# The second FFN projection as one Strassen step, with its operand sums made during the first projection

## The chip, the cores and the metric

The kernel is one program on one core of a Trainium2 chip. Its time is the device time in microseconds (us) of one execution: 2015.59 us, the median of 3 runs (2013.15 to 2016.86). The engines are TensorE (PE in the rows; PEld is its weight load), VectorE (DVE), ScalarE (ACT), GpSimd (POOL) and SyncE (SP), which here only issues DMA transfers. The granted clock of TensorE has two levels, 1.2 and 2.4 GHz; in the rows 1.00 is the upper one and 0.50 the lower.

## The reference

One layer of a decoder trunk works on x with 1024 tokens and 1024 columns. Four token mixers come first; then a feed-forward network (FFN) and a gated embedding:

```
h2 = rmsnorm(x, g_pre_ffn[l])
gt, up = jnp.split(h2 @ w_ffn_in[l], 2, axis=-1)
x = x + rmsnorm((jax.nn.silu(gt) * up) @ w_ffn_out[l], g_post_ffn[l])
e = p[l] @ w_ple_in[l]
ge = jax.nn.sigmoid(rmsnorm(x, g_ple[l]) @ w_ple_gate[l])
x = x + ge * e
```

The hidden width is 2816, that is 22 tiles of 128, counted by f. Everything is float32.

## The kernel before, in words

Every matrix product is made of three matmuls in fp32r (`mm3`, L162): each operand is kept as a high part and the rest, and the kernel adds high by high, high by low and low by high. The high part is a copy on ScalarE (L74), the low part a subtraction on VectorE (L75). One matmul has a stationary tile of 128x128 and moves 512 columns.

The first projection (`ffn_in`, `ffn_in_fast`) works through f = 0 to 21 with tokens in two halves of 512. f = 0 and 1 are done plainly, 96 matmuls each: gate and up for both halves (names `fg`, `fu`), with the weights `whi`/`wlo` in two rotating buffers. Beside them `sums_of_h2` (L898) loads quarters of the normalised input (`r`, L907), forms their sums (L909 to L912) and splits them into `th`/`tl`. From f = 2 on, one Strassen step makes gate and up of a tile by 7 products of 12 matmuls (name `fw`). The sums of the weights (`sw`) and their splits (`wsh`/`wsl`) are made by `prep(f + 1)`, one step of it after each product of f. The finished hidden tile is split and stored to DRAM (`hidh`, `hidl`), 256 KB at a time.

The second projection (`ffn_out`) takes the hidden tiles in chunks of four f (the last has two). For a chunk it loads `fhh`, `fhl` and the rows of the second weight (512 KB each), and for each of 8 token tiles and 2 column halves it makes 12 matmuls into one bank (name `fo`); the sum is kept in `acc` in SBUF, copied by ScalarE for the first chunk (L1016), added by VectorE for the others (L1018). The last chunk is interleaved with the output norm and the gated embedding.

The order in each engine's queue is not that of the code: when the program is built, a planner that estimates durations and arrivals places the instructions, and each engine then works strictly in that order. Tiles of a kind share a pool of buffers (38 of 4 KB per partition for `u` tiles, 6 for `t`, 8 for `t2`, 2 each for `raw`, `whi`, `wlo`), and who takes a buffer waits for its last reader.

Of the kernel before, what the change touches and what calls it, by code (L numbers as in the profile page):

```python
# [27 lines left out]
CF_K = 31  # L28
LAG = 2
NF = HID // P  # L30
PLAIN, CHUNK = 2, 4
EPS = 1e-6
LAM_INIT = 0.8 - 0.6 * math.exp(0.0)
C_Q, C_K, C_V, C_LX, C_LG, C_SB, C_SC, C_SX, C_CA, C_CG, C_GATE = [512 * i for i in range(11)]
# [5 lines left out]
def tile_hybrid_layer(ctx: ExitStack, tc: tile.TileContext, a):  # L40
# [826 lines left out]
    acc = [None] * NT  # L867
    w1 = a["w_ffn_in"][0]
    w2 = a["w_ffn_out"][0]
    chunks = [list(range(c, min(c + CHUNK, NF))) for c in range(0, NF, CHUNK)]  # L870
    hidh, hidl = [dram.tile([NF, P, S], F32, name=n) for n in ("hidh", "hidl")]

    def keep_hidden(f, h, v):
        s = slice(h * HF, (h + 1) * HF)
        hh, hl = t2tile("fh", F32R), t2tile("fl", F32R)
        split(hh, hl, v)
        nc.sync.dma_start(hidh[f, :, s], hh.bitcast(F32))
        nc.sync.dma_start(hidl[f, :, s], hl.bitcast(F32))

    def ffn_in(f):  # L880

        gh, gl = load_w(w1[:, f * P:(f + 1) * P])
        uh, ul = load_w(w1[:, HID + f * P:HID + (f + 1) * P])
        for h in range(2):
            pg = mmtile("fg")
            mm3(pg, [(gh[:, k, :], gl[:, k, :], h2T.his(k, h * HF, HF), h2T.los(k, h * HF, HF)) for k in range(NK)])
            g = t2tile("fsilu")
            nc.scalar.activation(g, pg, AF.Silu)
            pu = mmtile("fu")
            mm3(pu, [(uh[:, k, :], ul[:, k, :], h2T.his(k, h * HF, HF), h2T.los(k, h * HF, HF)) for k in range(NK)])  # L890
            nc.vector.tensor_mul(g, pu, g)
            keep_hidden(f, h, g)

# [71 lines left out]
    def ffn_in_fast(f, ops, todo):  # L965
        x = {"B11": quarter(0, 0), "B21": quarter(1, 0), "B22": quarter(1, 1),
             "T1": tops[0], "T2": tops[1], "T3": tops[2], "T4": tops[3]}
        b0, b1, b2, b3 = banks(f, "fw")

        def product(ps, w, m, start):  # L970
            wh, wl = ops[w]
            mm3(ps, [(wh[:, k, :], wl[:, k, :], x[m][k // 2][0][:, k % 2, :], x[m][k // 2][1][:, k % 2, :])
                     for k in range(4)], start, True, not start)
            if todo:
                todo.pop(0)()

        product(b0, "A11", "B11", True)
        p1 = t2tile("p1")
        nc.scalar.activation(p1, b0, AF.Copy)
        product(b1, "S2", "T2", True)  # L980
        u2 = t2tile("u2")
        nc.vector.tensor_add(u2, b1, p1)
        product(b2, "S3", "T3", True)
        v = t2tile("v")
        nc.vector.tensor_add(v, b2, u2)
        product(b3, "S1", "T1", True)
        nc.vector.tensor_add(v, b3, v)
        product(b0, "A12", "B21", False)
        g0 = gp.tile([P, HF], F32, tag="g", name=nm("fsilu"))
        nc.scalar.activation(g0, b0, AF.Silu)  # L990
        product(b2, "A22", "T4", False)
        c21 = t2tile("c21")
        nc.vector.tensor_add(c21, b2, u2)
        nc.vector.tensor_mul(c21, c21, g0)
        keep_hidden(f, 0, c21)
        product(b3, "S4", "B22", False)
        run(todo)
        nc.vector.tensor_add(u2, b3, u2)
        g1 = gp.tile([P, HF], F32, tag="g", name=nm("fsilu"))
        nc.scalar.activation(g1, u2, AF.Silu)  # L1000
        nc.vector.tensor_mul(v, v, g1)
        keep_hidden(f, 1, v)

    def ffn_out(ci, hid, wts):
        first, last = ci == 0, ci == len(chunks) - 1
        n = len(hid)
        for t in range(NT):
            ts = slice(t * P, (t + 1) * P)
            if first:
                acc[t] = utile([P, D], F32, "acc")  # L1010
            for c in range(2):
                cs = slice(c * HF, (c + 1) * HF)
                ps = pta.tile([P, HF], F32, tag="tr" if c == 1 and not last else "ta", name=nm("fo"))
                mm3(ps, [(hid[i][0][:, ts], hid[i][1][:, ts], wts[i][0][:, cs], wts[i][1][:, cs]) for i in range(n)])
                if first:
                    nc.scalar.activation(acc[t][:, cs], ps, AF.Copy)  # L1016
                else:
                    nc.vector.tensor_add(acc[t][:, cs], acc[t][:, cs], ps)  # L1018
            if last:
                if t < 2:  # L1020
                    wpg.extend(load_row(a["w_ple_gate"][0][k * P:(k + 1) * P, :], [P, D]) for k in range(4 * t, 4 * t + 4))
                ffn_post(t)
                if t >= LAG:
                    ple(t - LAG)
        if last:
            for t in range(NT - LAG, NT):
                ple(t)
# [53 lines left out]
    for ci, fs in enumerate(chunks):  # L1081
        hid, wts = [], []
        for f in fs:
            hh, hl = utile([P, S], F32R, "fhh"), utile([P, S], F32R, "fhl")
            nc.sync.dma_start(hh.bitcast(F32), hidh[f])
            nc.sync.dma_start(hl.bitcast(F32), hidl[f])
            hid.append((hh, hl))
            wts.append(load_row(w2[f * P:(f + 1) * P, :], [P, D]))
        if ci < len(chunks) - 1:
            ffn_out(ci, hid, wts)  # L1090
# [41 lines left out]
```

## Time and profile before

| what | value |
|---|---|
| median of 3 runs | 2015.59 us |
| the profiled execution | 2013.32 us, span 2011.5 us |
| TensorE busy | 1971.7 us, 98% |
| VectorE busy | 1159.8 us, 58% |
| ScalarE busy | 755.8 us, 38% |
| mean granted clock | 0.997 |
| bytes moved by DMA | 181.10 MB, mean 90 GB/s |

The profile is of one execution. Its span is from the first to the last instruction; 1.8 us of the execution lie outside it. A matmul's row tells how long it is in the array, but matmuls overlap, so TensorE's pace is the distance between starts, and a stretch of rows without idle time gives it as its length over its count. An engine that is not the bottleneck may idle at no cost.

### The profile page before, as it was taken

The numbers are of one execution on the slowest core, as the hardware profiler recorded it, in microseconds if no ns is written. First come the engines' busy times: TensorE is split into PE (matmuls) and PEld (weight loads), VectorE is DVE, ScalarE is ACT, GpSimd is POOL, SyncE is SP. The second block draws the span as 40 slices with busy tenths as digits, with TensorE's granted clock in tenths as the row PEclk, the third lists the DMA queues.
The fourth block names the chain that finished last, engine by engine and source line by source line (L and its number), as shares of the span: only waits on it lengthen the run. The fifth ranks groups of instructions, "written<-read, shape, count | busy, mean of one in ns | idle before, by whom it ended". The sixth has DMA issues, their size and how long they took to land.

```text
span 2011.5 us, 23079 instructions
## 1 busy us (share of the span) xinstructions
PE 1971.7 (98%) x9165; PEld 1635.4 (81%) x9165; DVE 1159.8 (58%) x1663; ACT 755.8 (38%) x1251; POOL 53.7 (3%) x33
## 2 busy tenths in 40 slices
PE   6999999999999999999999999999999999999999
PEld 5878887888887888878888878888888888788887
DVE  4487679697957323464233454876666651433574
ACT  5456564511115212464122344433333332201274
POOL 1011111000000000000000000000000000000000
PEclk9999999999999999999999999999999999999999
DMA  6110111021110112112111354533333344543232
GB/s 238 61 58 22 32 32 32 22 58 48 53 53 27 58 47 63 43 32 63 48 48 47 101 183 132 176 126 109 101 126 105 105 159 165 193 180 150 85 126 94
DMA packets 185610, 181.10 MB, mean 90 GB/s; under 512 B 8112, under 2 KB 151409, under 8 KB 185502
## 3 DMA queue, kind: packets, MB, share of 16 engines
q1 hardware_dynamic: 180320, 171.47, 26.0%
q10 hardware_dynamic: 5182, 8.16, 1.2%
q8 instruction: 72, 1.18, 0.2%
q14 instruction: 36, 0.29, 0.0%
HBM read 138.96 MB, written 40.63 MB: 89 GB/s over the span
## 4 chain that ended last, share of the span: by engine, by line
PE 79%; DVE 8%; DMA 2%; ACT 2%; issue 1%; POOL 0%; SPq 0%; POOLq 0%; DVEq 0%; ACTq 0%
PE fw L171 6%; PE fw L173 6%; PE fw L174 6%; PE pg L174 5%; PE pg L173 5%; PE pg L171 5%; PE pz L171 5%; PE pz L173 5%; PE pz L174 5%; PE fo L174 4%; PE fo L173 4%; PE fo L171 4%; PE pb L174 3%; PE pb L171 3%; PE pb L173 3%; DVE cfc L473 1%
## 5 line engine op out<-in xcount | busy, mean ns | idle before, releaser
L75 DVE TENSOR_TENSOR wlo<-raw,whi 128x1024 fp32r<-128x1024 f32 x110 | 117.3, 1067 | 273.5 <-ACT whi L74 273.4
L74 ACT ACTIVATE whi<-raw 128x1024 fp32r<-128x1024 f32 (+1 forms) x128 | 121.9, 953 | 370.4 <-PE pg L173 123.4
L171 PE MATMUL pz<-hTh,whi 128*128 128x512 f32 x576 | 228.0, 396 | 2.0 <-ACT scc L609 1.7
L173 PE MATMUL pz<-hTl,whi 128*128 128x512 f32 x576 | 226.8, 394 | 0.0
L174 PE MATMUL pz<-hTh,wlo 128*128 128x512 f32 x576 | 226.5, 393 | 0.0
L174 PE MATMUL pg<-hTh,wlo 128*128 128x512 f32 x512 | 199.1, 389 | 0.5 <-DVE wlo L75 0.5
L173 PE MATMUL pg<-hTl,whi 128*128 128x512 f32 x512 | 199.3, 389 | 0.0
L171 PE MATMUL pg<-hTh,whi 128*128 128x512 f32 x512 | 199.2, 389 | 0.0
L473 DVE SCALAR_TENSOR_TENSOR cfc<-cfu,cvec,cfc 128x994 f32<-128x994 f32 (+14 forms) x120 | 161.3, 1344 | 2.6
L171 PE MATMUL fo<-rwh,fhh 128*128 128x512 f32 x352 | 136.4, 390 | 0.7 <-DMA fhh<-hidh 0.5
L173 PE MATMUL fo<-rwl,fhh 128*128 128x512 f32 x352 | 136.4, 390 | 0.2
L174 PE MATMUL fo<-rwh,fhl 128*128 128x512 f32 x352 | 135.8, 389 | 0.0
L171 PEld LDWEIGHTS pz<-hTh,whi 128*128 128x128 f32 x576 | 108.9, 189 | 25.2 <-ACT scc L609 2.2
L174 PEld LDWEIGHTS pz<-hTh,wlo 128*128 128x128 f32 x576 | 108.9, 189 | 22.8 <-issue 0.5
L173 PEld LDWEIGHTS pz<-hTl,whi 128*128 128x128 f32 x576 | 108.9, 189 | 22.3 <-issue 0.7
L1018 DVE TENSOR_TENSOR acc<-acc,fo 128x512 f32<-128x512 f32 x80 | 54.6, 687 | 104.1 <-PE fo L174 104.1
L174 PEld LDWEIGHTS pg<-hTh,wlo 128*128 128x128 f32 x512 | 96.1, 188 | 20.9 <-DVE wlo L75 0.9
L171 PEld LDWEIGHTS pg<-hTh,whi 128*128 128x128 f32 x512 | 96.1, 188 | 19.9
L173 PEld LDWEIGHTS pg<-hTl,whi 128*128 128x128 f32 x512 | 96.1, 188 | 19.8
L74 ACT ACTIVATE rwh<-raw 128x1024 fp32r<-128x1024 f32 x40 | 41.8, 1058 | 175.8 <-PE fo L173 109.7
L171 PE MATMUL fw<-th,wsh 128*128 128x512 f32 x240 | 93.4, 389 | 0.0
L173 PE MATMUL fw<-tl,wsh 128*128 128x512 f32 x240 | 93.4, 389 | 0.0
(319 smaller groups left out, 4181.0 us busy)
## 6 DMA issues: line engine op xcount, KB each, us to landing
raw<-in_w_in_dram SPq DMA_DIRECT2D x72, 512.0 KB, 3.6
raw<-in_w_ffn_in_dram SPq DMA_DIRECT2D x44, 512.0 KB, 3.7
hidh<-fh SPq DMA_DIRECT2D x44, 256.0 KB, 2.8
hidl<-fl SPq DMA_DIRECT2D x44, 256.0 KB, 2.2
raw<-in_w_ffn_out_dram SPq DMA_DIRECT2D x22, 512.0 KB, 7.8
fhh<-hidh SPq DMA_DIRECT2D x22, 512.0 KB, 3.6
fhl<-hidl SPq DMA_DIRECT2D x22, 512.0 KB, 7.9
raw<-in_w_branch_dram SPq DMA_DIRECT2D x32, 256.0 KB, 2.8
```

The lines of the kernel that those rows point to most:

```text
L74: nc.scalar.activation(dst_hi, src, AF.Copy)
L75: (eng or nc.vector).tensor_sub(dst_lo, src, dst_hi.bitcast(F32))
L171: nc.tensor.matmul(ps, lhsT=lh, rhs=rh, start=start and i == 0, stop=False, skip_group_check=onto)
L173: nc.tensor.matmul(ps, lhsT=lh, rhs=rl, start=False, stop=False, skip_group_check=onto)
L174: nc.tensor.matmul(ps, lhsT=ll, rhs=rh, start=False, stop=stop and i == n - 1, skip_group_check=onto)
L473: nc.vector.scalar_tensor_tensor(o, in0=src[:, a0 - sh:t0 + n - sh], scalar=cv(name, j, k), in1=o, op0=ALU.mult, op1=ALU.add)
L1018: nc.vector.tensor_add(acc[t][:, cs], acc[t][:, cs], ps)
```

## The change

The first ten pairs of tiles f (0 to 19) of the second projection are done by one Strassen step: tokens in two halves, output columns in two halves, and the two f of a pair as the two halves of the inner dimension. For a pair, 7 products take the place of 8; each has 4 token tiles of 3 matmuls. Pairs are taken in groups of 3, 3 and 4, whose products are summed in the same bank. The seven left operands of a pair (A11, A12, A22 and four sums HS1 to HS4 of the hidden quarters) are made and split in the first projection, in steps (`spare`) of which one is taken after each product, and stored to DRAM (`sums_d`, 36.7 MB, where `hidh` and `hidl` held 21.0 MB for these twenty tiles). The second projection (`out_fast`) loads one of them (`so`, 512 KB) for each pair and product, forms and splits the weight's sums (`to`) as it goes, and adds the products into `acc` and, for two of them, `accu`. The tiles f = 20 and 21 stay as they were (`out_last`). The hidden tile now stays in SBUF in a `t` buffer (`hid`) until its pair's sums are made.

```diff
-PLAIN, CHUNK = 2, 4
+PLAIN, NP = 2, 10
+GROUPS = (3, 3, 4)
...
+    sums_d = dram.tile([7, NP, P, 2, HF], F32, name="sums_d")
+    last_d = dram.tile([NF - 2 * NP, 2, P, S], F32, name="last_d")
+    A11, A12, A22, HS1, HS2, HS3, HS4 = range(7)
+    hidden, spare = {}, []
+    def keep(dst, v):
         hh, hl = t2tile("fh", F32R), t2tile("fl", F32R)
         split(hh, hl, v)
-        nc.sync.dma_start(hidh[f, :, s], hh.bitcast(F32))
-        nc.sync.dma_start(hidl[f, :, s], hl.bitcast(F32))
+        nc.sync.dma_start(dst[0], hh.bitcast(F32))
+        nc.sync.dma_start(dst[1], hl.bitcast(F32))
+    def keep_hidden(f, h):
+        n, second = divmod(f, 2)
...
+        if h == 0:
+            spare.append(lambda: put(A12 if second else A11, hidden[f][:, 0]))
+        elif second:
+            x, y, z = hidden[f - 1], hidden[f], []
+            def first():
+                z.append(utile([P, 2, HF], F32, "hs"))
+                nc.vector.tensor_add(z[0][:, 0], x[:, 1], y[:, 1])
+                nc.vector.tensor_sub(x[:, 1], x[:, 0], x[:, 1])
+            def then():
+                nc.vector.tensor_sub(z[0][:, 1], z[0][:, 0], x[:, 0])
+                nc.vector.tensor_sub(y[:, 0], y[:, 0], z[0][:, 1])
+            spare.extend([lambda: put(A22, y[:, 1]), first, lambda: put(HS3, x[:, 1]), then,
+                          lambda: put(HS1, z[0][:, 0]), lambda: put(HS2, z[0][:, 1]), lambda: put(HS4, y[:, 0])])
     def ffn_in(f):
...
+        hidden[f] = ttile(S, "hid").rearrange("p (u c) -> p u c", u=2)
...
-            nc.vector.tensor_mul(g, pu, g)
-            keep_hidden(f, h, g)
+            nc.vector.tensor_mul(hidden[f][:, h], pu, g)
+            keep_hidden(f, h)
...
             if todo:
                 todo.pop(0)()
+            if spare:
+                spare.pop(0)()
...
+    order = (("P1", A11), ("P6", HS2), ("P2", A12), ("P7", HS3), ("P5", HS1), ("P4", A22), ("P3", HS4))
+    onto = {"P2": "P1", "P4": "P7", "P3": "P5"}
...
+    def out_ops(g, name, i):
+        for n in members[g]:
+            so = utile([P, 2, HF], F32R, "so")
+            nc.sync.dma_start(so.bitcast(F32), sums_d[i, n])
...
+            to = utile([P, 2, HF], F32R, "to")
+            split(to[:, 0], to[:, 1], src[0][:, src[1]])
...
+    def out_fast():
+        seq = [(g, name, i) for g in range(len(GROUPS)) for name, i in order]
...
+        for m, (g, name, i) in enumerate(seq):
+            ops = nxt
+            if name == "P4" and g + 1 < len(GROUPS):
+                load_raw(g + 1)
+            if m + 1 < len(seq):
+                nxt = out_ops(*seq[m + 1])
...
+            for t in range(NH):
+                ts = slice(t * P, (t + 1) * P)
+                mm3(ps[t], [(s[:, 0, ts], s[:, 1, ts], w[:, 0], w[:, 1]) for s, w in ops], not cont, True, cont)
...
+                if g == 0 and name not in ("P6", "P5"):
+                    nc.scalar.activation(dst, ps[t], AF.Copy)
+                else:
+                    nc.vector.tensor_add(dst, dst, ps[t])
+                if g == len(GROUPS) - 1 and name in ("P4", "P5", "P3"):
+                    nc.vector.tensor_add(dst, dst, accu[t])
```

The change also moves instructions. Three places at the handover from the plain tiles (f = 0, 1) to the fast ones (f = 2) are shown, of before and of the change. On VectorE, this is the stretch ahead of the second product of f = 2, before (`r` are the input's sums of the second set, `wlo` the low part of the plain first operand's weights of f = 2, `wsl` that of the second product's, `fu` the up half of f = 1):

```order
L911 TENSOR_TENSOR r_1683_9857<-r_1683_9857,r_1681_9853 128x1024
L75 TENSOR_TENSOR tl_1686_9866<-r_1681_9853,th_1685_9865 128x1024
L912 TENSOR_TENSOR r_1684_9859<-r_1684_9859,r_1683_9857 128x1024
L891 TENSOR_TENSOR fsilu_1672_9760<-fu_1673_9762,fsilu_1672_9760 128x512
L75 TENSOR_TENSOR tl_1688_9870<-r_1683_9857,th_1687_9869 128x1024
L75 TENSOR_TENSOR tl_1690_9874<-r_1682_9855,th_1689_9873 128x1024
...
L939 TENSOR_TENSOR sw_1696_9886<-raw_1693_9881,sw_1695_9885 128x512
L75 TENSOR_TENSOR wlo_1698_9890<-raw_1693_9881,whi_1697_9889 128x1024
L75 TENSOR_TENSOR wsl_1700_9896<-sw_1695_9885,wsh_1699_9895 128x1024
```

and the same work on VectorE in the change:

```order
L942 TENSOR_TENSOR r_1675_9831<-r_1676_9833,r_1675_9831 128x1024
L76 TENSOR_TENSOR wlo_1692_9868<-raw_1687_9859,whi_1691_9867 128x1024
L943 TENSOR_TENSOR r_1676_9833<-r_1677_9835,r_1676_9833 128x1024
L76 TENSOR_TENSOR tl_1680_9844<-r_1675_9831,th_1679_9843 128x1024
L944 TENSOR_TENSOR r_1677_9835<-r_1677_9835,r_1675_9831 128x1024
L924 TENSOR_TENSOR hid_1668_9724<-fu_1674_9805,fsilu_1673_9803 128x512
L945 TENSOR_TENSOR r_1678_9837<-r_1678_9837,r_1677_9835 128x1024
L76 TENSOR_TENSOR tl_1682_9848<-r_1677_9835,th_1681_9847 128x1024
...
L971 TENSOR_TENSOR sw_1689_9863<-sw_1689_9863,raw_1687_9859 128x512
...
L76 TENSOR_TENSOR wsl_1694_9874<-sw_1689_9863,wsh_1693_9873 128x1024
```

`wlo` has moved from behind the second set of input sums to a place after the first of them; between it and `wsl` now stand 13 other instructions, where there was none. On SP, the DMA issues before:

```order
L907 DMA r_1681_9853<-h2d_8746 128x2x512
L907 DMA r_1682_9855<-h2d_8746 128x2x512
L907 DMA r_1683_9857<-h2d_8746 128x2x512
L927 DMA raw_1693_9881<-in_w_ffn_in_dram 128x8x128
L907 DMA r_1684_9859<-h2d_8746 128x2x512
```

and in the change:

```order
L960 DMA raw_1687_9859<-in_w_ffn_in_dram 128x8x128
L960 DMA raw_1688_9861<-in_w_ffn_in_dram 128x8x128
L940 DMA r_1675_9831<-h2d_8746 128x2x512
L940 DMA r_1676_9833<-h2d_8746 128x2x512
L940 DMA r_1677_9835<-h2d_8746 128x2x512
L940 DMA r_1678_9837<-h2d_8746 128x2x512
```

The second set of input quarters is now issued behind both weight tiles of f = 2 (the two `hid` tiles hold two of the six `t` buffers that it used). On TensorE, this is the end of the first product of f = 2 and the start of the second (before, `fw_1704` is the bank of the first and `fw_1705` that of the second; in the change `fw_1698` and `fw_1699`; `h2Th_1471` belongs to the fifth product, which adds onto the first one's bank). Before:

```order
L171 MATMUL fw_1704_9906<-h2Th_1470_8731,whi_1697_9889 128x512
L173 MATMUL fw_1704_9906<-h2Tl_1478_8739,whi_1697_9889 128x512
L174 MATMUL fw_1704_9906<-h2Th_1470_8731,wlo_1698_9890 128x512
L171 MATMUL fw_1705_9907<-th_1659_9711,wsh_1699_9895 128x512
L173 MATMUL fw_1705_9907<-tl_1660_9712,wsh_1699_9895 128x512
L174 MATMUL fw_1705_9907<-th_1659_9711,wsl_1700_9896 128x512
```

and in the change:

```order
L175 MATMUL fw_1698_9884<-h2Th_1470_8731,wlo_1692_9868 128x512
L172 MATMUL fw_1698_9884<-h2Th_1471_8732,whi_1691_9867 128x512
L174 MATMUL fw_1698_9884<-h2Tl_1479_8740,whi_1691_9867 128x512
L172 MATMUL fw_1699_9885<-th_1656_9700,wsh_1693_9873 128x512
L174 MATMUL fw_1699_9885<-tl_1657_9701,wsh_1693_9873 128x512
L175 MATMUL fw_1698_9884<-h2Th_1471_8732,wlo_1692_9868 128x512
L175 MATMUL fw_1699_9885<-th_1656_9700,wsl_1694_9874 128x512
```

Three matmuls of the fifth product have moved ahead of the third matmul of the second, which is the first to read `wsl`.

## Rows read from the trace of the kernel before

**Rows 1.** The page: the span, and busy time per engine.
```profile
span 2011.5 us, 23079 instructions
PE 1971.7 (98%) x9165; PEld 1635.4 (81%) x9165; DVE 1159.8 (58%) x1663; ACT 755.8 (38%) x1251; POOL 53.7 (3%) x33
```

**Rows 2.** Stretches (each engine's busy us and count, granted clock, DMA): both projections.
```profile
core 0: us, PE busy (x) PEld busy (x) DVE busy (x) ACT busy (x) POOL busy (x), PEclk, DMA share, GB/s
1400.00:1437.90 37.90, 37.90 (x169) 31.39 (x168) 25.46 (x35) 13.36 (x18) 0.00 (x0) 1.00 0.34 111
1724.00:1832.30 108.30, 108.30 (x479) 89.71 (x478) 41.54 (x54) 11.46 (x11) 0.00 (x0) 1.00 0.45 171
1669.90:1886.70 216.80, 216.11 (x951) 178.06 (x950) 69.25 (x89) 32.03 (x39) 0.00 (x0) 1.00 0.40 149
```

**Rows 3.** Groups by form in 1724.00 to 1832.30.
```profile
L174 PE MATMUL fo<-rwh,fhl 128*128 128x512 f32 x160 | 62.2, 389 | 0.0
L1018 DVE TENSOR_TENSOR acc<-acc,fo 128x512 f32<-128x512 f32 x43 | 29.4, 687 | 66.5 <-PE fo L174 66.5
```

**Rows 4.** Timeline of TensorE at the handover to f = 2.
```profile
1283.20 0.39 PE L171 MATMUL fu<-h2Th,whi 128*128 128x512 f32 x1
...
1288.64 0.39 PE L171 MATMUL fw<-h2Th,whi 128*128 128x512 f32 x1
1288.86 0.39 PE L173 MATMUL fw<-h2Tl,whi 128*128 128x512 f32 x1
...
1291.36 0.39 PE L171 MATMUL fw<-th,wsh 128*128 128x512 f32 x1
...
1291.81 0.39 PE L174 MATMUL fw<-th,wsl 128*128 128x512 f32 x1
```

**Rows 5.** Timeline of VectorE at the handover.
```profile
1277.54 1.22 DVE L911 TENSOR_TENSOR r<-r,r 128x1024 f32<-128x1024 f32 x1
1278.68 1.22 DVE L75 TENSOR_TENSOR tl<-r,th 128x1024 fp32r<-128x1024 f32 x1
...
1285.55 0.69 DVE L933 TENSOR_TENSOR sw<-raw,raw 128x512 f32<-128x512 f32 x1
1286.15 0.69 DVE L938 TENSOR_TENSOR sw<-sw,raw 128x512 f32<-128x512 f32 x1
...
1287.49 1.22 DVE L75 TENSOR_TENSOR wlo<-raw,whi 128x1024 fp32r<-128x1024 f32 x1
1288.62 2.35 DVE L75 TENSOR_TENSOR wsl<-sw,wsh 128x1024 fp32r<-128x1024 f32 x2
```

**Rows 6.** Timeline of ScalarE at the handover.
```profile
1283.22 1.06 ACT L74 ACTIVATE whi<-raw 128x1024 fp32r<-128x1024 f32 x1
```

**Rows 7.** The stretch of the handover.
```profile
1268.30:1288.60 20.30, 20.30 (x91) 16.84 (x90) 18.57 (x20) 9.63 (x12) 0.00 (x0) 1.00 0.41 130
```

**Rows 8.** Timeline of TensorE after an idle time near the kernel's start.
```profile
27.81 0.79 PE L171 MATMUL pe<-whi,pTh 128*128 128x512 f32 x1 [4.84 <-ACT e L220]
28.40 0.63 PE L173 MATMUL pe<-wlo,pTh 128*128 128x512 f32 x1
28.83 0.63 PE L174 MATMUL pe<-whi,pTl 128*128 128x512 f32 x1
...
33.45 0.40 PE L173 MATMUL pe<-wlo,pTh 128*128 128x512 f32 x1
33.69 0.40 PE L174 MATMUL pe<-whi,pTl 128*128 128x512 f32 x1
```

**Rows 9.** Stretches around that idle time.
```profile
23.00:28.00 5.00, 0.19 (x1) 0.19 (x2) 2.42 (x4) 4.33 (x8) 0.00 (x0) 0.81 0.94 318
28.00:32.00 4.00, 4.00 (x10) 3.02 (x11) 1.73 (x2) 1.47 (x3) 0.94 (x1) 0.50 1.00 364
18.00:20.00 2.00, 2.00 (x14) 1.74 (x13) 0.62 (x2) 1.22 (x3) 0.95 (x1) 1.00 1.01 396
```

**Rows 10.** DMA issues: count, KB each, median us to landing.
```profile
raw<-in_w_ffn_out_dram SPq DMA_DIRECT2D x22, 512.0 KB, 7.8
```

More of the change, by code (lines that the diff above doesn't have):

```diff
@@ L869, in tile_hybrid_layer, with put @@
     w2 = a["w_ffn_out"][0]
[L870 to L874, printed above, removed]
+    sums_d = dram.tile([7, NP, P, 2, HF], F32, name="sums_d")
[3 more added lines that the diff above has]
+    def keep(dst, v):
         hh, hl = t2tile("fh", F32R), t2tile("fl", F32R)
         split(hh, hl, v)
-        nc.sync.dma_start(hidh[f, :, s], hh.bitcast(F32))
-        nc.sync.dma_start(hidl[f, :, s], hl.bitcast(F32))
+        nc.sync.dma_start(dst[0], hh.bitcast(F32))
+        nc.sync.dma_start(dst[1], hl.bitcast(F32))
+    def keep_hidden(f, h):
+        n, second = divmod(f, 2)
+        if n >= NP:
+            s = slice(h * HF, (h + 1) * HF)
+            spare.append(lambda: keep([last_d[f - 2 * NP, u, :, s] for u in range(2)], hidden[f][:, h]))
+            return
+        def put(i, v):
+            keep([sums_d[i, n, :, u, :] for u in range(2)], v)
+        if h == 0:
[11 more added lines that the diff above has]
+                          lambda: put(HS1, z[0][:, 0]), lambda: put(HS2, z[0][:, 1]), lambda: put(HS4, y[:, 0])])
     def ffn_in(f):
@@ L975, in product @@
                 todo.pop(0)()
+            if spare:
+                spare.pop(0)()
+        hv = ttile(S, "hid").rearrange("p (u c) -> p u c", u=2)
+        hidden[f] = hv
         product(b0, "A11", "B11", True)
@@ L991, in ffn_in_fast @@
         product(b2, "A22", "T4", False)
[L992 to L995, printed above, removed]
+        nc.vector.tensor_add(hv[:, 0], b2, u2)
+        nc.vector.tensor_mul(hv[:, 0], hv[:, 0], g0)
+        keep_hidden(f, 0)
         product(b3, "S4", "B22", False)
@@ L1000, in ffn_in_fast @@
         nc.scalar.activation(g1, u2, AF.Silu)
[L1001 to L1006, printed above, removed]
+        nc.vector.tensor_mul(hv[:, 1], v, g1)
+        keep_hidden(f, 1)
+    NH = NT // 2
+    order = (("P1", A11), ("P6", HS2), ("P2", A12), ("P7", HS3), ("P5", HS1), ("P4", A22), ("P3", HS4))
+    onto = {"P2": "P1", "P4": "P7", "P3": "P5"}
+    sets = {"P1": 0, "P6": 1, "P7": 1, "P5": 0}
@@ new lines, in tile_hybrid_layer, with load_raw @@
+    raws, mids = {}, {}
+    def load_raw(g):
+        for n in members[g]:
+            raws[n] = []
+            for f in (2 * n, 2 * n + 1):
+                raws[n].append(utile([P, 2, HF], F32, "w2r"))
+                nc.sync.dma_start(raws[n][-1], w2[f * P:(f + 1) * P, :].rearrange("p (u c) -> p u c", u=2))
+    def out_ops(g, name, i):
+        ops = []
+        for n in members[g]:
+            so = utile([P, 2, HF], F32R, "so")
+            nc.sync.dma_start(so.bitcast(F32), sums_d[i, n])
+            ops.append([so])
+        for n, op in zip(members[g], ops):
+            (r0, r1) = raws[n]
+            if name == "P6":
+                m = mids[n] = ttile(D, "tt").rearrange("p (u c) -> p u c", u=2)
+                nc.vector.tensor_sub(m[:, 0], r0[:, 1], r0[:, 0])
+                nc.vector.tensor_sub(m[:, 1], r1[:, 1], m[:, 0])
+            elif name == "P7":
+                nc.vector.tensor_sub(r0[:, 1], r1[:, 1], r0[:, 1])
+            elif name == "P4":
+                nc.vector.tensor_sub(mids[n][:, 1], r1[:, 0], mids[n][:, 1])
+            src = {"P1": (r0, 0), "P2": (r1, 0), "P7": (r0, 1), "P3": (r1, 1)}.get(name)
+            if src is None:
+                src = (mids[n], 0 if name == "P5" else 1)
+            to = utile([P, 2, HF], F32R, "to")
+            split(to[:, 0], to[:, 1], src[0][:, src[1]])
+            op.append(to)
+        return ops
@@ new lines, in tile_hybrid_layer @@
+    members, n0 = [], 0
+    for n in GROUPS:
+        members.append(list(range(n0, n0 + n)))
+        n0 += n
+    accu = []
+    def out_fast():
+        seq = [(g, name, i) for g in range(len(GROUPS)) for name, i in order]
+        for t in range(NT):
+            acc[t] = utile([P, D], F32, "acc")
+        for t in range(0, NH, 2):
+            u = utile([P, 2, HF], F32, "accu")
+            accu.extend([u[:, 0], u[:, 1]])
+        lo, hi = slice(0, HF), slice(HF, D)
+        load_raw(0)
+        nxt = out_ops(*seq[0])
+        held = {}
+        for m, (g, name, i) in enumerate(seq):
[4 more added lines that the diff above has]
+                nxt = out_ops(*seq[m + 1])
+            cont = name in onto
+            if cont:
+                ps = held[onto[name]]
+            else:
+                ps = held[name] = banks(g + sets[name], "fo")
+            for t in range(NH):
+                ts = slice(t * P, (t + 1) * P)
+                mm3(ps[t], [(s[:, 0, ts], s[:, 1, ts], w[:, 0], w[:, 1]) for s, w in ops], not cont, True, cont)
+                dst = {"P1": accu[t], "P6": accu[t], "P2": acc[t][:, lo], "P7": acc[NH + t][:, hi],
+                       "P5": acc[NH + t][:, hi], "P4": acc[NH + t][:, lo], "P3": acc[t][:, hi]}[name]
+                if g == 0 and name not in ("P6", "P5"):
+                    nc.scalar.activation(dst, ps[t], AF.Copy)
+                else:
+                    nc.vector.tensor_add(dst, dst, ps[t])
+                if g == len(GROUPS) - 1 and name in ("P4", "P5", "P3"):
+                    nc.vector.tensor_add(dst, dst, accu[t])
@@ L1007, in ffn_out, with out_last @@
+    def out_last(hid, wts):
         for t in range(NT):
             ts = slice(t * P, (t + 1) * P)
-            if first:
-                acc[t] = utile([P, D], F32, "acc")
             for c in range(2):
                 cs = slice(c * HF, (c + 1) * HF)
[L1013 to L1027, printed above, removed]
+                ps = pta.tile([P, HF], F32, tag="ta", name=nm("fo"))
+                mm3(ps, [(h[0][:, ts], h[1][:, ts], w[0][:, cs], w[1][:, cs]) for h, w in zip(hid, wts)])
@@ L1029, in tile_hybrid_layer @@
+                nc.vector.tensor_add(acc[t][:, cs], acc[t][:, cs], ps)
+            if t < 2:
+                wpg.extend(load_row(a["w_ple_gate"][0][k * P:(k + 1) * P, :], [P, D]) for k in range(4 * t, 4 * t + 4))
+            ffn_post(t)
+            if t >= LAG:
+                ple(t - LAG)
+        for t in range(NT - LAG, NT):
+            ple(t)
     h3 = []
@@ L1080, in tile_hybrid_layer @@
         ops = nxt
[L1081 to L1090, printed above, removed]
+    run(spare)
+    out_fast()
+    hid, wts = [], []
+    for f in range(2 * NP, NF):
+        hl = [utile([P, S], F32R, "fhh"), utile([P, S], F32R, "fhl")]
+        for u in range(2):
+            nc.sync.dma_start(hl[u].bitcast(F32), last_d[f - 2 * NP, u])
+        hid.append(hl)
+        wts.append(load_row(w2[f * P:(f + 1) * P, :], [P, D]))
     g_post2 = bcast(a["g_post_ffn"], D, "g_post_ffn")
@@ L1093, in tile_hybrid_layer @@
     wpg = []
-    ffn_out(len(chunks) - 1, hid, wts)
+    out_last(hid, wts)
     psB.close()
```

## The prediction

> **What bounds the kernel now.** I read the page first: TensorE is busy 1971.7 of 2011.5 us, 98% [rows 1]; time can only be saved by taking work from it or lost by making it wait. Then I read both FFN projections as stretches. In 1400.00 to 1437.90, two tiles f of the first projection, TensorE is busy for the whole of it with 169 matmuls, VectorE for 25.46 us and ScalarE for 13.36; in 1724.00 to 1832.30, in the second, 479 matmuls fill 108.30 us and VectorE has 41.54 [rows 2]. So both stages run at TensorE's pace. That pace is not a matmul's 389 ns [rows 3]: starts lie 0.22 to 0.23 us apart (1288.64, 1288.86) [rows 4], and 108.30/479 = 0.226 us each. Last I looked at the place where the change alters the queues most, the handover to f = 2.
>
> **The gain.** For a pair of f the old projection makes 2 f x 8 token tiles x 2 column halves x 3 = 96 matmuls, the new one 7 products x 4 x 3 = 84. Ten pairs save 120, at 0.226 us = 27.1 us. This presupposes that every stage still runs at TensorE's pace, so I go through them.
>
> **First projection, f = 2 to 21.** A pair gets seven more instructions on VectorE: three splits (7 x 512 columns instead of 4) and four sums. They run back to back 0.60 us apart (1285.55, 1286.15), with 0.69 us in each row [rows 5]: 7 x 0.69 = 4.8 us. VectorE goes from 25.46 to 30.3 of 37.9 us, 80% [rows 2]. They come one per product, in the f that ends a pair's wait, so one f carries seven extra splits and the other few. Before, the handover ran 18.57 of 20.30 us on VectorE, 91%, without TensorE idling there [rows 7]; I take 0, since 7.6 of VectorE's 12.4 idle us per pair remain. No gain is possible here, as TensorE has no idle time to give back; a badly placed instruction could cost about one split's 0.69 us per pair, 7 us in ten pairs. The extra stores (six of 256 KB, 1.57 MB per 37.9 us, 41 GB/s) bring 111 to 152 GB/s, below the 171 that the second projection moves with TensorE full [rows 2].
>
> **The handover to f = 2.** On VectorE `wlo` of f = 2 now comes after the first of the second set's input sums, and needs `whi`, whose buffer is free when the gate half of f = 1 ends. In the trace that is at 1283.20, where the last up half starts [rows 4], and ScalarE makes `whi` at 1283.22 in 1.06 us [rows 6]. So VectorE, strictly in order, does nothing of what follows before 1284.3. From there I add up: `wlo`, the sum L943, a `tl` and the sum L944 (1.14 us each by the starts 1277.54 and 1278.68 [rows 5]) end at 1288.9. The product of `fu` needs the last up half, which ends with the start of `fw` at 1288.64 plus a matmul's 0.39: 0.60 more from 1289.0, 1289.7. The sum L945 and three `tl` are 4 x 1.14, 1294.2; three `sw` 1.8, 1296.0. Now ScalarE can make `wsh`, 1.06 us, 1297.1, while VectorE does a `fl` and a `sw` to 1297.2; `wsl` takes 1.22 to 1298.4. TensorE in this order has done by then the 12 matmuls of product 1, three of a later product and two of product 2, and waits for `wsl`. Without a wait these 17 would have ended at 1288.64 + 17 x 0.226 = 1292.5. Loss: 5.9 us, rounded to 6.0. In before the same two stood at 1291.36 and 1291.81, no wait [rows 4]. The wait has a short first piece, since the fifth product's matmuls need the copy of the first bank, and a long one of some 4 us ahead of `wsh`, from about 1293 to 1297.1. Behind it nothing else is late: `wsl` of product 3 follows 2.5 us later, and product 2 lasts 2.7. Some us earlier `wlo` of f = 1 also comes later, behind three `tl`; there TensorE's order has three gate matmuls moved ahead, which covers it. Bounds of the loss: 0 (the operands come as early as in before) and 11 us: the second set of quarters is issued behind the second weight tile, whose buffer is free with `wlo` of f = 1, at about 1273.5; 7.8 us to landing [rows 10] is 1281, in time, but twice that is 1289, 5 us late. I take 6.0, the replay of the rows.
>
> **The clock.** A piece of 4 us without matmuls is near the only such place in the trace: TensorE idled 4.84 us before 27.81, and then started matmuls 0.43 us apart until past 31 us, where 33.45 and 33.69 are 0.24 apart again [rows 8]; the granted clock is 0.50 in 28 to 32 us, the lower level [rows 9]. In those 4 us TensorE did ten records' work, so it lost about half of them, 2 us; with the tail 2.2. I take 2.2; the bounds are 0 (the clock holds) and 4.4 (twice the row).
> The Trainium skill, page "TensorE: Matmul & The Clock Gate", section "HAM oscillation — how this bites in real kernels", says that an idle stretch of TensorE can drop its clock, so that work after it starts cold, each time again. The row agrees (0.50 after 4.84 us of idling); by the rule the sum carries the 2.2, and without it the time would be 2.2 us shorter.
>
> **Second projection.** Transfers: 70 operands and 20 weight tiles of 0.524 MB are 47.2 MB in 840 x 0.226 = 190 us, 249 GB/s; before, this stage moved 149 in the mean and 171 where busiest, at a DMA share of 0.45 [rows 2]. At 18.00 to 20.00 the queues moved 396 GB/s at a share of 1.01 [rows 9], so 249 is some 0.63 of that. A product of three pairs is 36 matmuls, 8.1 us; buffers let a load start about two products ahead, 16 us, against 7.8 us to landing [rows 10]. Where the next group's six weight tiles are issued ahead of a product's loads, 12 transfers (6.3 MB) have some 24 us, 262 GB/s: the tightest place, twice. VectorE, for a group of three pairs, has 21 splits, 12 sums and 28 additions, each 0.69 us in its row [rows 3, 5] and 0.60 apart, 37 of 57 us. I take 1 us; bounds 0 and 10 (a load's 7.8 us late at one group's start, and smaller waits). The last stage, f = 20, 21 and the embedding, has the same work: 0.
>
> **Sum.** 27.1 - 0 - 6.0 - 2.2 - 1.0 = 17.9 us. The profiled execution, 2013.32 us (its span 2011.5 and 1.8 around it), would become 1995.4. It is 2.3 below the median of 2015.59; on the median the forecast is 1997.7.
>
> **Rivals.**
> - The wait at f = 2 does not show: the full gain less 1, 1989.5. For it, the planner's places are estimates; against it, `wlo` waits for an event on TensorE, and what follows is fixed work. 11%.
> - Small waits throughout: VectorE at 80% in the first projection delays TensorE by up to 1 us per pair, 10 us, or the second loses as much: 2003 to 2010. Speaks for it: the spare steps stand in queues that TensorE waits for. Against: the 7.6 us of idle per pair. 14%.
> - Slower: the second projection is bound by its loads. At 171 GB/s, the highest rate that this stage showed, 47.2 MB take 276 us, against 216.8 before: +59, and with the 8.2 of the handover 2083. It decides below 47.2/(216.8 - 8.2) = 226 GB/s. For it: every load stands in SP's one queue, where one that waits for a buffer holds up those behind it. Against: 396 GB/s in rows 9, with TensorE's own work going on. 7%.
> - The pace is the 389 ns of a row: gain 46.7, 1978. The starts rule it out: 1%.
> The Trainium skill, page "DMA: Bandwidth & Descriptors", section "Bandwidth", asks for transfers of 1 MiB or more for three quarters of the peak; these are of 512 KB. It speaks for the slower rival, which by its row of 1 MB, 341 GB/s, would still not decide; the 396 GB/s of rows 9, made of loads of that size, speak against it.
>
> **Chances and range.** Forecast 67%, own range 1993 to 2003 (losses at 5 to 15 us); 11% at about 1989.5, 14% at 2003 to 2010, 7% slower, 1% at 1978. A range of 1989 to 2007 leaves out the slower case, the end of the small waits, and some of the first rival: 2 in 10. A measurement tells 0.2%, 4 us, from no change: faster is everything below 2011.6, 67 + 11 + 1 and 9 of the 14 for the small waits, 0.88; same 0.05, the other 5 of these 14, should the waits of both stages add up; slower 0.07.
>
> **What would show it.** In the profile after: 120 fewer matmuls; `fo` starts 0.226 apart from first to last; at f = 2 one gap of TensorE ahead of its third matmul that reads `wsl`, released by VectorE, some 6 us in all, and matmuls 0.43 apart for a few us after it; no other gap of over 1 us up to the last stage. Gaps before `fo` released by a load of `so` or by `to` would show the third rival at work, gaps before `fw` in pairs the second. If no gap stands at f = 2, the step on VectorE's order is wrong.

## The result, and the profile after

The change takes 1992.80 us, the median of 4 runs (1990.62 to 1993.24), against 2014.37 us of before in the same comparison: a ratio of 0.9893 with a 95% interval of 0.988 to 0.9906, 21.6 us less. The forecast was 1997.7 us with 1989 to 2007. The profiled execution took 1993.24 us, 20.1 less than that of before, where 17.9 were forecast.

The page of the change, span and busy time (against [rows 1]):

```profile
span 1991.4 us, 23345 instructions
PE 1944.7 (98%) x9045; PEld 1613.2 (81%) x9045; DVE 1243.3 (62%) x1835; ACT 787.4 (40%) x1335; POOL 53.7 (3%) x33
```

TensorE is still busy 98%, with 120 matmuls fewer, and VectorE has more work. Stretches of the change, columns as in [rows 2]: the first projection, the busiest part of the second, and a later one:

```profile
core 0: us, PE busy (x) PEld busy (x) DVE busy (x) ACT busy (x) POOL busy (x), PEclk, DMA share, GB/s
1400.00:1475.00 75.00, 75.00 (x333) 62.12 (x332) 57.42 (x82) 28.91 (x42) 0.00 (x0) 1.00 0.46 153
1677.50:1741.00 63.50, 62.30 (x275) 51.25 (x274) 35.76 (x59) 27.63 (x51) 0.00 (x0) 1.00 0.78 289
1741.00:1805.00 64.00, 64.00 (x284) 53.05 (x283) 46.51 (x75) 13.19 (x23) 0.00 (x0) 1.00 0.68 248
```

TensorE has no idle time in the first projection (333 matmuls in 75.00 us, 0.225 us each), with VectorE at 57.42/75 = 77%, where 80% were forecast. In the second projection the transfers run at 289 GB/s first and then at 248, where 249 were forecast; only 1.2 us of TensorE are idle.

At the handover to f = 2, TensorE's timeline of the change answers to [rows 4]; the bracket is the idle time ahead of an instruction and what ended it:

```profile
1289.19 0.39 PE L172 MATMUL fw<-h2Th,whi 128*128 128x512 f32 x1
...
1291.69 0.39 PE L175 MATMUL fw<-h2Th,wlo 128*128 128x512 f32 x1
1293.03 0.50 PE L172 MATMUL fw<-h2Th,whi 128*128 128x512 f32 x1 [0.95 <-ACT p L1016]
1293.36 0.40 PE L174 MATMUL fw<-h2Tl,whi 128*128 128x512 f32 x1
1297.59 0.79 PE L172 MATMUL fw<-th,wsh 128*128 128x512 f32 x1 [3.83 <-ACT wsh L75]
1298.18 0.63 PE L174 MATMUL fw<-tl,wsh 128*128 128x512 f32 x1
1298.61 0.63 PE L175 MATMUL fw<-h2Th,wlo 128*128 128x512 f32 x1
1299.04 0.63 PE L175 MATMUL fw<-th,wsl 128*128 128x512 f32 x1
...
1301.60 0.63 PE L175 MATMUL fw<-th,wsl 128*128 128x512 f32 x1
1302.02 0.53 PE L172 MATMUL fw<-th,wsh 128*128 128x512 f32 x1
1302.39 0.40 PE L174 MATMUL fw<-tl,wsh 128*128 128x512 f32 x1
1302.63 0.39 PE L175 MATMUL fw<-th,wsl 128*128 128x512 f32 x1
```

There are two waits, 0.95 and 3.83 us, and then starts 0.43 us apart up to 1302.02. The prediction's steps had them at these places; its list of signs named a gap ahead of `wsl`'s reader, where none stands. In addition, f = 2 itself began 0.55 us later than in before, and `wsl`'s first reader, forecast for 1298.4, starts at 1299.04. The granted clock in that stretch (against [rows 9]):

```profile
1293.00:1297.50 4.50, 0.73 (x2) 0.30 (x2) 4.50 (x7) 1.02 (x2) 0.00 (x0) 0.78 0.00 0
1297.50:1302.00 4.50, 4.41 (x10) 3.33 (x11) 4.46 (x7) 2.02 (x4) 0.00 (x0) 0.50 0.82 249
```

0.50 is the lower level, 1.2 GHz. VectorE there; the first line is of before (it belongs ahead of those in [rows 5]), the others are of the change:

```profile
1272.79 1.22 DVE L909 TENSOR_TENSOR r<-r,r 128x1024 f32<-128x1024 f32 x1
...
1279.26 0.69 DVE L924 TENSOR_TENSOR hid<-fu,fsilu 128x512 f32<-128x512 f32 x1 [5.44 <-PE fu L175]
1281.54 1.22 DVE L942 TENSOR_TENSOR r<-r,r 128x1024 f32<-128x1024 f32 x1 [1.59 <-DMA r<-h2d]
1284.87 1.22 DVE L76 TENSOR_TENSOR wlo<-raw,whi 128x1024 fp32r<-128x1024 f32 x1 [2.10 <-ACT whi L75]
...
1289.42 0.69 DVE L924 TENSOR_TENSOR hid<-fu,fsilu 128x512 f32<-128x512 f32 x1
1290.02 1.22 DVE L945 TENSOR_TENSOR r<-r,r 128x1024 f32<-128x1024 f32 x1
1291.15 3.49 DVE L76 TENSOR_TENSOR tl<-r,th 128x1024 fp32r<-128x1024 f32 x3
1294.56 0.69 DVE L965 TENSOR_TENSOR sw<-raw 128x512 f32<-128x512 f32 x1
1295.16 0.69 DVE L966 TENSOR_TENSOR sw<-raw,raw 128x512 f32<-128x512 f32 x1
1295.76 0.69 DVE L971 TENSOR_TENSOR sw<-sw,raw 128x512 f32<-128x512 f32 x1
```

ScalarE's split behind the last of these, and SP's issues, both of the change:

```profile
1296.48 1.06 ACT L75 ACTIVATE wsh<-sw 128x1024 fp32r<-128x1024 f32 x1 [3.51 <-DVE sw L971]
```

```profile
1264.05 10.21 SPq L960 DMA_DIRECT2D raw<-in_w_ffn_in_dram  x2
1274.32 2.15 SPq L940 DMA_DIRECT2D r<-h2d  x4
```

What to see: SP spent 10.21 us on the two weight tiles of f = 2, and issued the second set of input quarters only behind them, at 1274.32 (in before the last of that set was issued at 1268.3). VectorE, which in before made that set's sums from 1272.79 on, idled 5.44 us here until a matmul of f = 1 was done, then 1.59 us for the loads, then 2.10 us for `whi`. From 1289.42 on it works without a pause up to the sum that `wsh` is made of.

The stages, read from the timelines as the start of the first instruction of each kind (us):

| from, to | before | the change | difference |
|---|---|---|---|
| start to first `fg` | 1243.99 | 1244.31 | +0.32 |
| `fg` to first `fw` (f = 0, 1) | 44.65 | 44.88 | +0.23 |
| `fw` to first `fo` (f = 2 to 21) | 381.24 | 388.34 | +7.10 |
| `fo` to first `pgate` (second projection) | 233.20 | 206.00 | -27.20 |
| `pgate` to last `pgate` (output stage) | 104.05 | 103.38 | -0.67 |

The sum is -20.2; the rest, behind the last `pgate`, is +0.2. In the runs below, the start of `fg` lay between 1239.9 and 1246.7 us in kernels whose code ahead of it is the same, while a stage that two kernels share agreed within 0.03 us (`fo` to `pgate`) to 1.1 us (the output stage, 103.91 and 104.99 us in the two kernels with eight `t` buffers below). So the stages tell more than the whole time.

### The profile page after: what moved, and what is told of

Read it like the earlier page. It is cut to its first block, busy times and chain, and to the rows that moved or that the text cites. A ratio compares the mean times of both kernels' runs of the same rounds, so it can differ in the third digit from the quotient of the medians.

```text
span 1991.4 us, 23345 instructions
## 1 busy us (share of the span) xinstructions
PE 1944.7 (98%) x9045; PEld 1613.2 (81%) x9045; DVE 1243.3 (62%) x1835; ACT 787.4 (40%) x1335; POOL 53.7 (3%) x33
## 4 chain that ended last, share of the span: by engine, by line
PE 82%; DVE 7%; ACT 2%; DMA 1%; issue 1%; POOL 0%; POOLq 0%; ACTq 0%; DVEq 0%
PE fw L175 6%; PE fw L172 6%; PE fw L174 6%; PE pg L175 6%; PE pg L174 6%; PE pg L172 6%; PE pz L172 5%; PE pz L174 5%; PE pz L175 5%; PE fo L172 3%; PE fo L175 3%; PE fo L174 3%; PE pb L175 3%; PE pb L174 3%; PE pb L172 3%; PE pgate L172 1%
## 5 line engine op out<-in xcount | busy, mean ns | idle before, releaser
L172 PE MATMUL fo<-to,so 128*128 128x512 f32 x280 | 108.5, 390 | 1.2 <-ACT to L75 1.2
L174 PE MATMUL fo<-to,so 128*128 128x512 f32 x280 | 109.0, 389 | 0.0
L175 PE MATMUL fo<-to,so 128*128 128x512 f32 x280 | 109.0, 389 | 0.0
L175 PE MATMUL fw<-th,wsl 128*128 128x512 f32 x240 | 94.2, 392 | 0.0
L448 ACT ACTIVATE gate<-pg,gvec 128x512 f32<-128x512 f32 x64 | 43.5, 681 | 127.3 <-PE pg L175 122.2
```

The costliest lines, as they stand in the source:

```text
L448: nc.scalar.activation(g, pg, AF.Sigmoid, bias=gvec[:, b * NK + d:b * NK + d + 1])
```

## The experiments

The theory behind the prediction: 120 matmuls at TensorE's pace are gained, and 7 us are lost at f = 2 to a wait and the lower clock. Rivals: the wait comes from the added work itself, the clock is not the cause of the slow starts, small waits are spread over the first projection, or the second one is limited by its loads. Medians are of single sets of runs; each set has its own runs of before.

**The hidden tiles of f = 0 and 1 in other buffers.**

```diff
-        hidden[f] = ttile(S, "hid").rearrange("p (u c) -> p u c", u=2)
+        hidden[f] = utile([P, 2, HF], F32, "hid")
```

> The hidden tiles of f = 0 and 1 take buffers of the 38 (u) instead of two of the six t buffers; nothing else is changed. VectorE's order then has the low part of the weights (wlo) of f = 2 behind the second set of input sums again, and TensorE's order has its products of 12 undivided. Theory (the wait at f = 2 is made by that order, 4.8 us of idle time and about 2.3 us at the lower clock): both go, no matmul of f = 2 waits over 0.5 us, the clock stays at 1.00 from 1288 to 1304, and the time falls by 7 us to about 1985.7. Rival (the added work on VectorE makes the wait, whatever the order): a wait of 4 us or more remains at f = 2 or moves to the products after it, and the time stays at 1991 to 1994.

Measured: 1986.83 us, ratio 0.9869 (0.9853 to 0.9886); `fw` to `fo` 381.41 us, 6.9 less than the change. SP and TensorE in this kernel:

```profile
1253.90 11.09 SPq L940 DMA_DIRECT2D r<-h2d  x6
1265.74 0.37 SPq L960 DMA_DIRECT2D raw<-in_w_ffn_in_dram  x1
1268.01 0.36 SPq L940 DMA_DIRECT2D r<-h2d  x1
1270.88 17.53 SPq L960 DMA_DIRECT2D raw<-in_w_ffn_in_dram  x2
```

```profile
1287.42 0.39 PE L174 MATMUL fw<-h2Tl,whi 128*128 128x512 f32 x1
1288.06 0.50 PE L175 MATMUL fw<-h2Th,wlo 128*128 128x512 f32 x1 [0.25 <-DVE wlo L76]
```

Six of the input quarters are now issued in one row from 1253.90 on and the last at 1268.01, between the weight tiles; the only wait left is 0.25 us. The added work of the first projection is unchanged, so the rival falls. This is also the fastest kernel measured that computes the layer: faster than the change by 6.0 us in the medians. The edit moves SP's, VectorE's and TensorE's order at once, so it shows that the place of the two tiles makes the loss, and not yet by which of these orders.

**Filling the wait with matmuls.**

```diff
         product(b0, "A11", "B11", True)
+        if f == PLAIN:
+            fill = pta.tile([P, HF], F32, tag="ta", name=nm("fill"))
+            for i in range(6):
+                mm3(fill, [(x["B11"][0][0][:, 0, 0:P], x["B11"][0][1][:, 0, 0:P], x["B11"][0][0][:, 1, :], x["B11"][0][1][:, 1, :])])
```

> The change as it is, with 18 matmuls more behind the first product of f = 2, into a free bank that nothing reads (4.1 us of TensorE at 0.2265). They stand in the two waits and give no operand earlier. Theory (2.3 of the 7.1 us lost at f = 2 are the lower clock after the wait, not the wait): the granted clock stays at 1.00, the second product starts at the same 1297.6 or at most 0.3 us later, the first matmuls after it are 0.23 apart instead of 0.43, and the time falls by about 2 us, to 1990.8. Rival (the slow starts after the wait come from late operands, wsl and what follows): spacing 0.43 remains and the time stays within 0.5 us of 1992.8, or rises by up to 4 us.

Measured: 1990.87 us, ratio 0.9893 (0.9875 to 0.9911); `fw` to `fo` 385.62 us, 2.72 less than the change. The end of the fill and the start of the second product, and the clock:

```profile
1295.98 0.50 PE L172 MATMUL fw<-th,wsh 128*128 128x512 f32 x1 [0.30 <-ACT wsh L75]
1296.32 0.39 PE L174 MATMUL fw<-tl,wsh 128*128 128x512 f32 x1
1296.55 0.40 PE L175 MATMUL fw<-h2Th,wlo 128*128 128x512 f32 x1
```

```profile
1291.00:1296.00 5.00, 4.70 (x22) 3.57 (x20) 5.00 (x8) 1.49 (x3) 0.00 (x0) 1.00 0.00 0
1296.00:1302.00 6.00, 6.00 (x26) 4.79 (x27) 5.17 (x8) 3.46 (x5) 0.00 (x0) 1.00 0.81 248
```

`wsh` released TensorE 8.40 us after the first `fw` (1287.58 to 1295.98), exactly as in the change (1289.19 to 1297.59): no operand came earlier. The clock held at 1.00, and starts behind the wait are 0.23 apart. Of the 2.72 us, 0.68 are three matmuls of the fifth product more than in the change that the order placed ahead of the wait; about 2.0 are the clock. The ratio to before is the same as the change's, so the whole time does not show the gain; the stage and the starts do. The rival falls.

**Without the added work of the first projection** (on the first experiment's kernel).

```diff
-            spare.extend([lambda: put(A22, y[:, 1]), first, lambda: put(HS3, x[:, 1]), then,
-                          lambda: put(HS1, z[0][:, 0]), lambda: put(HS2, z[0][:, 1]), lambda: put(HS4, y[:, 0])])
+            spare.extend([lambda: put(A22, y[:, 1]), lambda: put(HS1, x[:, 1])])
...
-            nc.sync.dma_start(so.bitcast(F32), sums_d[i, n])
+            nc.sync.dma_start(so.bitcast(F32), sums_d[min(i, HS1), n])
```

> As the kernel with the hidden tiles of f = 0 and 1 in u buffers, but without the extra work of the first projection: of the seven operands of a pair only four are split and stored (as many as before the change) and none is summed; the second projection loads these four in place of the seven, so its loads, matmuls and weight work are the same and the output is not the reference's. Left out per pair: 3 splits and 4 sums on VectorE (4.8 us), 3 copies on ScalarE, 6 stores. Theory (TensorE never waits for this work): the same time as that kernel within 1 us, f = 3 to 21 at the same pace. Rival (small waits throughout, up to 1 us per pair): 3 to 10 us less.

Measured: 1986.45 us, ratio 0.9871 (0.9856 to 0.9886). `fw` to `fo` is 380.80 against 381.41 us. The same stretch in this kernel and in the first experiment's:

```profile
1400.00:1475.00 75.00, 75.00 (x332) 62.15 (x331) 48.01 (x68) 25.06 (x35) 0.00 (x0) 1.00 0.35 112
```

```profile
1400.00:1475.00 75.00, 75.00 (x332) 62.12 (x331) 56.94 (x82) 28.79 (x42) 0.00 (x0) 1.00 0.46 155
```

VectorE has 48.01 us of work instead of 56.94, TensorE 332 matmuls in 75 us in both. All the sums and splits cost TensorE 0.6 us, some 0.5 of them where the first experiment's kernel waits at f = 2: there are no small waits throughout.

**More transfers in the second projection.**

```diff
+    dup_d = dram.tile([7, NP, P, 2, HF], F32, name="dup_d")
...
             nc.sync.dma_start(so.bitcast(F32), sums_d[i, n])
+            if True:
+                nc.gpsimd.dma_start(dup_d[i, n], so.bitcast(F32))
```

> The change as it is, and GpSimd, otherwise idle here, also stores each operand of the second projection that was loaded back to another place in DRAM: 70 stores of 0.524 MB more, 84 MB in place of 47 in that stage. Theory (the stage has DMA room up to about 396 GB/s; it uses some 257): at most 84 MB at 380 to 400 GB/s, 210 to 221 us in place of 192, so 18 to 29 us more, about 2011 to 2022, with waits of fo for so. Rival (what limits loads here is SP's one queue and its waits for buffers, not the bytes): under 5 us more.

Measured: 2018.96 us, ratio 1.0028 (1.0018 to 1.0039), 26 us more than the change; `fo` to `pgate` 231.37 us. Stretches, and the two longest of the waits of TensorE from the first `fo` on (engine, line, what it waited for, us, times, longest):

```profile
1677.00:1741.00 64.00, 60.94 (x257) 49.91 (x256) 31.95 (x52) 25.39 (x47) 10.67 (x21) 0.95 1.03 415
1800.00:1870.00 70.00, 68.88 (x304) 56.73 (x304) 35.63 (x55) 13.10 (x22) 13.84 (x26) 1.00 1.03 419
```

```profile
PE fo L172 <- DVE acc L1131: 12.4, 1, 12.4
PE fo L172 <- DMA so<-sums_d: 4.2, 2, 3.1
```

The queues run full, 415 and 419 GB/s at a share of 1.03, so the change's 289 and 248 GB/s leave room. The rival of under 5 us falls; but the added stores also hold the `so` buffers longer (SP waited 14.8 us in all for them), and this run does not part that from the bytes. The place was missed: of the 25.4 us by which `fo` to `pgate` is longer, 18 are waits and some 5 are 26 starts at the lower clock; only 4.2 of the waits are for `so`, while 12.4 fall behind the ten pairs, where the gate's weights came late (one of these loads took 18.1 us from issue to landing, 7.3 in the change). The slower rival of the prediction needed less than 226 GB/s to decide; the stage can have 415.

**What makes the wait at f = 2: two more buffers, another order, or other weight buffers.** The first is `T_BUFS` 8 and `U_BUFS` 36; the second that and

```diff
-    run(todo)
+    run([todo[i] for i in (0, 1, 3, 4, 2, 5, 6)])
```

> The change with eight t buffers in place of six (and 36 u buffers in place of 38), so that the second set of input quarters needs no buffer of the first set. In VectorE's order the low part of the weights (wlo) of f = 2 still stands ahead of nine instructions that wsl comes behind, now after the sum L944 instead of L942. Theory (the place of wlo in VectorE's order makes the wait; the late loads only add to it): wsh is ready only about 1 us earlier, a wait of 3 to 4.5 us remains at f = 2 with matmuls 0.43 us apart behind it, and the time falls by 0 to 2 us, 1991 to 1993. Rival (the shortage of t buffers, and so the late loads of the second set, makes the wait): it goes, and the time falls by 6 to 7 us to 1986.

> As the kernel with eight t buffers, and in the preparation of f = 2 alone the split of the first operand's weights (whi, wlo) is written behind that of the second's (wsh, wsl); VectorE's order then has wlo behind wsl and all input sums, and TensorE's order begins f = 2 with parts of the second and third product. Theory (the place of wlo): no wait over 1 us at f = 2, no lower clock, about 7 us less than the change, 1985 to 1988. Rival (buffers and loads): the same time as the kernel with eight t buffers, whatever that is, within 1 us.

Measured: 2002.48 us, ratio 0.9945 (0.9928 to 0.9963), and 2006.08, ratio 0.9967 (0.9955 to 0.9978). Both expectations failed in the time: in these two kernels the plain tiles took 52.4 and 52.3 us instead of 44.9 (which of the two pools does that is not shown), so the whole time says nothing on the wait, and the wait itself has to be read. With eight buffers it is 0.71 us and 2.78 us (of `wsh`), within the 3 to 4.5 us of that run's theory; its rival had the wait gone, but the loads were still late there (issued from 1285.29 on), so the run did not put it to the test. Where `wlo` stands behind `wsl` there are two waits of 5.3 us in all, where the theory of that run had none. SP and ScalarE of the second:

```profile
1275.76 6.77 SPq L960 DMA_DIRECT2D raw<-in_w_ffn_in_dram  x2
1282.58 2.21 SPq L940 DMA_DIRECT2D r<-h2d  x4
```

```profile
1284.79 1.05 ACT L75 ACTIVATE th<-r 128x1024 fp32r<-128x1024 f32 x1
1295.00 1.06 ACT L75 ACTIVATE whi<-raw 128x1024 fp32r<-128x1024 f32 x1 [9.15 <-issue]
1296.44 1.05 ACT L75 ACTIVATE th<-r 128x1024 fp32r<-128x1024 f32 x1
```

Here too the second set is issued behind both weight tiles (1282.58), though with eight buffers its first two need none of the first set; why the planner left them there is open. Now ScalarE idles 9.15 us at `whi`, ahead of the set's `th`. Moving `wlo` alone does not take the wait away. The third run takes away what `whi` waits for:

```diff
-                if n == "g":
+                if n == "g" and f > PLAIN:
```

> The change as it is, but the first operand's weights of f = 2 are split into two u buffers of their own, so that nothing of f = 2 waits for the gate half of f = 1; SP's order is unchanged, with the second set of input quarters behind both weight tiles. VectorE's order then has that split behind the second set's sums, ahead of the split for the second product. Theory A (the place of wlo, which waits for the gate, in front of the input sums makes the wait): no wait over 1 us at f = 2, first fw to first fo in 381.5 us instead of 388.3, time 1986. Theory B (the second set's late loads make it: its sums and splits, 8.4 us of work behind the last up half of f = 1, stand in VectorE's queue ahead of the weights of f = 2, wherever wlo stands): the wait moves to the third matmul of the first product, about 6 us after the first, 387 to 388 us from fw to fo, time 1992 to 1993.

Measured: 1995.62 us, ratio 0.9913 (0.9898 to 0.9928). The start of f = 2:

```profile
1294.53 0.79 PE L172 MATMUL fw<-h2Th,wsh 128*128 128x512 f32 x1 [3.83 <-ACT wsh L75]
1295.12 0.63 PE L174 MATMUL fw<-h2Tl,wsh 128*128 128x512 f32 x1
1298.20 0.80 PE L175 MATMUL fw<-h2Th,wsl 128*128 128x512 f32 x1 [2.46 <-DVE wsl L76]
1298.80 0.63 PE L172 MATMUL fw<-h2Th,wsh 128*128 128x512 f32 x1
```

The waits are 3.83 us ahead of the first matmul and 2.46 ahead of the third, again with the lower clock. `fg` to `fw` took 48.94 us and `fw` to `fo` 385.54, 4.3 more than in before each. Theory A falls as far as `whi` goes. The run does not take away every wait for the gate: VectorE stood 2.47 us, ahead of the sum L943, at a split of the hidden tile whose copy ScalarE makes behind the gate's silu. Theory B stands in its mechanism; it placed the whole wait at the third matmul and missed that the first, which needs ScalarE's copy behind the set's `th`, is late too.

**The second projection's 1.2 us.** In the first experiment's kernel, the weight tiles of the next group were issued at the fifth product instead of the sixth (`name == "P5"`), and the groups were made 3, 4 and 3.

> As the kernel with the hidden tiles of f = 0 and 1 in u buffers, and the weight tiles of the next group are issued one product earlier (at the fifth product of a group instead of the sixth). Theory (the 1.2 us that TensorE waits for a weight split in the first group's last product come from six weight tiles that stand in SP's queue ahead of that product's loads): this wait goes, first fo to first pgate takes 204.8 us instead of 206.0, and the time is 1.2 us less than that kernel's 1986.8. Rival (the wait is ScalarE's, which copies the first group's sums out of PSUM besides): the wait stays and the time is the same within 0.5 us.

> As the kernel with the hidden tiles of f = 0 and 1 in u buffers, and the ten pairs in groups of 3, 4 and 3 instead of 3, 3 and 4. A product of the second group lasts 10.9 us instead of 8.2, and the first group's last product is followed by eight weight tiles instead of six. Theory (the 1.2 us wait in the first group's last product comes from the weight tiles ahead of its loads in SP's queue): it stays or grows by up to 2 us, the time is 1986 to 1989. Rival (it comes from the loads of the products after it): it goes, 1985.6.

Measured: 1989.50 us, ratio 0.9878 (0.9864 to 0.9893), and 1988.28 us, ratio 0.9873 (0.9856 to 0.9889). The theory for the earlier issue failed: a wait of 3.74 us for a weight split came in the product before, and `fo` to `pgate` took 210.12 us. With groups of 3, 4 and 3 the 1.21 us stayed, as that theory said, and the stage took 206.48. Neither is a gain; what makes the 1.2 us is left open.

## Why the prediction was right, and where not

- **The gain**, 27.1 us: 27.20 measured from `fo` to `pgate`. The term rests on the distance of starts (0.226 us), not on the 389 ns of a row, and that distance holds in every kernel here where TensorE does not wait and its granted clock is 1.00.
- **The first projection**, 0: 0.6 us by the run without the work.
- **The second projection**, a loss of 1.0: it has a wait of 1.2 us, but before lost as much: from `fo` to `pgate` stand 1013 matmuls of `fo` there and 893 now, at 0.2265 us 229.4 of 233.20 and 202.3 of 206.00, and some 3.7 us remain in both, eight small transposes among them. The term should have been set against the waits of before. The list of signs, too, had said that no other gap of over 1 us would stand. The 396 GB/s of [rows 9], set against the slower rival as made of 512 KB loads, had two stores of 256 KB issued among them; the run with more transfers shows the room with 512 KB alone.
- **The handover**, 6.0 for the wait and 2.2 for the clock: 7.10 us together. The replay placed the end of `wsh` (1297.1) and `wsl`'s reader (1298.4) within 0.1 us, once f = 2's later start is taken off. The sum was too large since 0.9 us of wait for `wsl` behind `wsh` and the slow matmuls after it lie over each other: measured are 0.95 + 3.83 us of idle time and 2.2 us for ten matmuls at 0.43 us.
- **Its cause** was told wrong. The step said that `wlo`, ahead of the input sums, holds VectorE, and that the second set, landing at about 1281, is in time. It did land there (VectorE took it at 1281.54). But in time for `wlo` is not in time for TensorE: work on VectorE and ScalarE remained behind the end of f = 1, 8.4 us in the change, and it remained where `wlo` stands behind `wsl` and where `whi` waits for nothing. The trace of the change shows the same: the last up half of f = 1 started its last matmul at 1288.97, so it was done at 1289.36, and VectorE took its product at 1289.42. Without the 2.10 us at `whi` VectorE would have waited there for the up half instead, so `whi` cost the chain at most 0.06 us. The replay's own steps have it so (the sums to end at 1288.9, the up half at 1289.0): its sum came near because it followed VectorE's order behind this product; that the reason was wrong did not matter to it, which is luck.
- **What the runs show in its place**: two `hid` tiles in `t` buffers make the loss, since one line that puts them elsewhere gives back 6.9 of the 7.1 us. The traces say by which way: SP issues the second set behind a weight tile that waits for its buffer, VectorE idles where it had worked, and the set's sums are left for behind f = 1. No run moves these loads alone, and two more `t` buffers did not bring them forward, so this way is read from the traces and not tested by itself.
- **The clock**, 2.2: the run with the fill shows it, about 2.0 us. The rule of the Trainium skill ("TensorE: Matmul & The Clock Gate", section "HAM oscillation — how this bites in real kernels"), that an idle stretch leaves the work after it cold, agrees with the 0.50 behind the 3.83 us of waiting.
- **The output stage** and the part ahead, 0: -0.67 and +0.55 us, within what runs of equal code differ by.
- **The total**: the profiled execution gained 2.2 us more than forecast, nearly all of it by the handover (1.1) and the second projection (1.0). The median lies 4.9 us below its forecast; the other 2.7 are which executions were profiled, that of before 2.3 us below its median and that of the change 0.4 above.

## What to carry to other kernels

When a change takes buffers for longer, look at what is loaded into the next ones and in which queue those loads now stand: a load behind an instruction that waits is late even if it lands before its first reader was due. When such a load feeds a chain, compare the chain's end with the reader that bounds the kernel, not with the next instruction in the queue. And compare stages between two common events rather than whole times, since the part ahead can drift by more than the effect.

## What was not expected of the hardware

- The queues moved 403 to 419 GB/s over 200 us at a share of 1.00 to 1.03 (the run with more transfers), loads and stores of 0.524 MB together, with TensorE at work beside them.
- TensorE's granted clock was 0.50, the lower level, behind a wait of 3.83 us in the change, and also behind one of 3.06 us in the run with more transfers (1725.20 to 1731.00). Where 2.78 us followed 0.71 us and two matmuls it was 0.57 in the mean of the next 3.4 us. Behind the 1.2 us in the second projection it stayed at 1.00.
